# Strassen's sums and products put into one order on two engines of a decoder kernel

## The chip, the cores and the metric

The kernel runs on one core of a Trainium2 chip. What counts is the device time of one execution in microseconds (us). A core has a matrix engine (PE), whose weight loads are told apart as PEld, three engines for elementwise work (VectorE, DVE; ScalarE, ACT; GpSimd, POOL) and a queue for transfers (SyncE, SP). Each engine works through its instructions in order. Where the program doesn't write an order out, a scheduler sets that of DVE, ACT, POOL and SP from priorities when the program is built.

## The reference

The reference computes two layers of a decoder on 256 tokens of width 1024. Each layer has a feed-forward network (FFN), a mixer and a second FFN, all followed by a layer norm. All arrays are float32. The change touches the FFNs alone; there are four.

```python
D_MODEL, SEQ, DEPTH, D_FF = 1024, 256, 2, 2816
def _swiglu(x, w1, w3, w2):
    return (jax.nn.silu(x @ w1) * (x @ w3)) @ w2
for l in range(DEPTH):
    h = _swiglu(x, ffn_w1[l, 0], ffn_w3[l, 0], ffn_w2[l, 0])
    x = _layernorm(ALPHA * x + 0.5 * h, ln_g[l, 0], ln_b[l, 0])
    h = _mixer(x, l, ...)
    x = _layernorm(ALPHA * x + h, ln_g[l, 1], ln_b[l, 1])
    h = _swiglu(x, ffn_w1[l, 1], ffn_w3[l, 1], ffn_w2[l, 1])
    x = _layernorm(ALPHA * x + 0.5 * h, ln_g[l, 2], ln_b[l, 2])
```

## The kernel before

**Numbers in two parts.** A float32 operand is split into a high part, which ACT copies into the rounded type (`whi`, L188 or L238), and a low part, which DVE finds as the number less its high part (`wlo`, L190 or L240). Each product is then three matmuls: high by high, low by high, high by low. The weights of both parts are made afresh from raw tiles of 128 x 2048 (1 MB), which SP loads (L164 for a tile in two halves, L166 for a whole one). `stream` (L169) does this for a tile: it loads it and issues, for each half of 1024 columns, the high part and the low part. `pieces` (L349) does it for a tile that is on chip already, through `split` (L236). The high and the low parts rotate through pools of eight buffers each (`hi_pool`, `lo_pool`).

**The front of an FFN.** silu(x w1) * (x w3) is made in blocks n = 0 to 4 of 512 columns, with two more columns of tiles (k = 16 and 17) by `gemm_a2`. Block 0 goes first, by `gemm_first` (L471) in the first FFN and by `gemm_b2` in the others. Then the loop at L875 goes through the blocks 1, 2 and 4 in twelve units of 24 matmuls (PE, L274). Between these units block 3 is made by Strassen's algorithm: the generator `seven` (L825) makes seven products of 12 matmuls each (PE, L362), and after the units 1, 2, 4, 6, 8, 9 and 10 the loop takes the next one (L887). PE's order is thus written out by hand. The products work on four quarters of the weights, w11, w12, w21 and w22, each a raw tile. They are, in this order: the first on w11; the crossed one on w21; the third on w11+w12; the fourth on that +w22; the fifth on w22; the sixth on w12+w22; the seventh on w11+w12+w22+w21, all up to sign conventions in the sums of x. The tiles of raw numbers are r1 (w11, then sums), r2 (w12, in two buffers of `hi_pool`) and r3 (w22, in two of `lo_pool`). Sums come about in two ways: `plus` (L344) adds two tiles on DVE, in two operations of 128 x 1024 (L346); `gather` (L338) issues two accumulating loads from POOL's queue (L341), which add the weights in memory onto the tile on chip. In the front, `plus` makes w11+w12 and +w22 in r1, and `gather` makes r2 = w12+w22 and the last r1 (+w21). The results are put together on DVE (L851, L852 and others); `sums_of_x` (through `strassen_sums`, L814 to L823, whose sums are L818) makes the sums of x on the side.

**The way to w2.** When a block is done, `turned` (L774) transposes it: `transposed` (L222) parts the two 16-bit halves of the numbers (L205 on ACT, L207 on POOL), a transfer from SP's queue transposes them (L211), and `joined` (L214) brings the halves together again, on ACT (L218) or on another engine (L220). Then the block is split into `h_hi` and `h_lo`. For blocks 3 and 4 the parting and the joining both run on ACT.

**The second weight, w2.** `gemm_seven` (L366) makes part of h w2 by Strassen's algorithm too, again seven products (PE, L362), and between them `between()` takes the streamed rest of the weights (PE, L391). There are `plus` and `gather` for the sums as in the front (`spare` stands for r2 and r3). Each product that goes into the residual is taken out of its bank by `ln.fold` (L593, on DVE), and the next product into that bank waits for it. At the end `held = list(rest(1))` (L434) streams the last weights, and the blocks of the second half follow.

**Small things beside.** `setup` (L527), started in the first front after its block 1 (n, t) = (1, 0) at L762, loads tables and the tokens from POOL's queue (L537), and after 12 beats (a beat is about the PE time of a unit's quarter) it issues a second part: small DVE operations and an Exp on ACT (L547), which changes ACT's table. `behind(ins)` (L148) makes an instruction be issued after another one on its engine; `beside(task, delay)` starts a side task in a number of beats.

Of the kernel before, what the change touches and what calls it, by code (L numbers as in the profile page):

```python
# [11 lines left out]
F32 = mybir.dt.float32  # L12
# [4 lines left out]
AF = mybir.ActivationFunctionType  # L17
# [37 lines left out]
def trunk(ctx, tc, x, xT, w13a, w13b, w2, wb, wqk, wu, wg, wgr, wbr, wbrr, wo, gateb, gatebr, sgug, sgub, sguwT, sgubias, lam, diffg,  # L55
# [28 lines left out]
    def slots(s, n, dtype=F32):  # L84

        return [act.tile([P, 512], dtype, tag="slot", name=name(s)) for _ in range((n + 1) // 2)]
# [58 lines left out]
    gate, behind_norm, sooner = [], [None], []  # L145
    latest, added, emptied, silu, turned_by, loaded, spread = [None, None], [None], [None], [None], [None], [None], [None]

    def behind(ins):  # L148

        return tc.issue_after(ins) if ins is not None else nullcontext()  # L150
# [18 lines left out]
    def stream(src, width=CH, sub=HC, lent=(), after=(None, None), pool=()):  # L169

        raw = fetch(src, width)
        out = []
        first = sooner.pop() if sooner else latest
        for o in range(0, width, HC):
            eng = G if o // HC in pool else V
            if o // HC in lent:
                hi, lo = ([act.tile([P, 512], F32R, tag="slot", name=name(n)) for _ in range(2)] for n in ("lhi", "llo"))
                at = [(hi[j], lo[j]) for j in range(2)]  # L180
            else:
                hi = hi_pool.tile([P, HC], F32R, tag="hi", name=name("whi"))
                lo = lo_pool.tile([P, HC], F32R, tag="lo", name=name("wlo"))
                at = [(hi[:, p : p + sub], lo[:, p : p + sub]) for p in range(0, HC, sub)]
            for p, (h, w) in zip(range(0, HC, sub), at):
                r = raw[:, o + p : o + p + sub]
                with behind(first[0]):
                    A.activation(h, r, AF.Copy)  # L188
                with behind(after[o // HC] or (first[1] if eng is V else None)):
                    eng.tensor_tensor(out=w, in0=r, in1=h.bitcast(F32), op=ALU.subtract)  # L190
            out.append((hi, lo))
        return out

# [149 lines left out]

    def plus(raw, more):  # L344
        for v, m in zip(halved(raw), halved(more)):
            V.tensor_tensor(out=v, in0=v, in1=m, op=ALU.add)  # L346
        return raw

    def pieces(raw):  # L349
        out = []  # L350
        for v in halved(raw):
            hi = hi_pool.tile([P, HC], F32R, tag="hi", name=name("whi"))
            lo = lo_pool.tile([P, HC], F32R, tag="lo", name=name("wlo"))
            split(hi, lo, v)
            out.append((hi, lo))
        return out

# [8 lines left out]
    def gemm_seven(src, xh, xl, sums, spare, ln, done):  # L366

        q = [[bank(), bank()], [side_bank(), bank()]]
        bx, bz = side_bank(), q[1][0]
        (w11, w21), (w12, w22) = ([s[:, o : o + CH] for o in (0, CH)] for s in src)

        def rest(c):  # L380
            for k in range(8, FT, 4):
                nk = min(4, FT - k)
                for j, piece in enumerate(stream(src[c][:, k * 512 : (k + nk) * 512], nk * 512)):
                    yield k + 2 * j, piece

        def rows(t, c, k0, piece, o=0, n=512):
            for j in range(2):
                k = k0 + j
                hi, lo = (w[:, j * 512 + o : j * 512 + o + n] for w in piece)
                for m, (y, x) in enumerate(((hi, xh), (lo, xh), (hi, xl))):  # L390
                    PE.matmul(q[c][t][:, :n] if o == 0 else more[:, :n], x(k, t), y,  # L391
                              start=k == 8 and m == 0 and (c, t) != (1, 0), stop=k == FT - 1 and m == 2, skip_group_check=True)
            beat(n / 1024)

        def block(t, k0):
            return tuple(lambda k, f=f: f(k0 + k, t) for f in (xh, xl))

        a11, a12, a22 = block(0, 0), block(0, 4), block(1, 4)
        first = rest(0)

        def between():
            k, piece = next(first)
            for t in range(NT):
                rows(t, 0, k, piece)

        r1 = fetch(w11)
        p1 = pieces(r1)
        r2 = fetch(w12, raw=spare[0])
        plus(r1, r2)
        product(bx, a11, p1, True, False)  # L410
        ln.fold(0, 0, bx, ALU.add, True)
        between()
        product(q[0][0], a12, pieces(fetch(w21)), False, False)
        gather(r2, w22)
        r3 = fetch(w22, raw=spare[1])
        between()
        product(bz, sums[0], pieces(r1), True, False)
        ln.fold(1, 1, bz, ALU.add, True)
        between()
        product(bx, sums[1], pieces(plus(r1, r3)), False, False)  # L420
        ln.fold(0, 1, bx, ALU.subtract, True)
        gather(r1, w21)
        between()
        product(bz, sums[3], pieces(r3), False, False)
        between()
        product(bx, sums[2], pieces(r2), False, False)
        ln.fold(1, 1, bx, ALU.subtract, False)
        between()
        product(bx, a22, pieces(r1), False, True)
        ln.fold(1, 0, bx, ALU.add, True)  # L430
        between()
        for t in range(NT):
            done(t, q[0][t], 0, 512)
        held = list(rest(1))  # L434
        cuts = ((0, 512),), (((0, 256), (256, 256)) if ln.last else ((0, 512),))
        for t in range(NT):
            for o, n in cuts[t]:
                more = bank() if o else None
                for k, piece in held:
                    rows(t, 1, k, piece, o, n)  # L440
                done(t, (more if o else q[1][t])[:, :n], 512 + o, n)
# [85 lines left out]
    def setup(after):  # L527
# [3 lines left out]
        for dst, src in ((x_tok[0], x[:P, :]), (x_tok[1], x[P:, :]), (cos_t, cosT), (sin_t, sinT), (dgs, diffg),  # L531
# [3 lines left out]
                first = first[:, 0]  # L535
            V.tensor_copy(first[:, :1], after)
            G.dma_start(dst, src)  # L537
        yield 12
        with behind(added[0]):
            V.tensor_scalar(out=gbh, in0=gbh, scalar1=0.5, scalar2=None, op0=ALU.mult)  # L540
        pr = s512("lampr").rearrange("p (l f d) -> p l f d", l=DEPTH, f=4)[:, :, :2]
# [189 lines left out]
    def ffn(l, f, i, norm, last=False):  # L731
# [14 lines left out]
        def front(n, wait):  # L746
# [10 lines left out]
            def done(t, ps):  # L757
                p = tiles[t]
                s = p[:, 1]
                added[0] = V.tensor_tensor(out=s, in0=s, in1=ps, op=ALU.mult).ins  # L760
                beside(turned(n, t, s, p[:, 0], wait[t]), 0)
                if norm is None and (n, t) == (1, 0):  # L762
                    beside(setup(s[:, :1]), 0)
            return gate_, done

# [8 lines left out]
        def turned(n, t, s, p, wait):  # L774
            lead = 3.5 if n == 0 and norm else 0
            to = slots("held", 2)[0] if n < 2 else p
            yield from transposed(s, p, s, lead, wait - lead, 2.6, A, to, A if n else G)
            yield 0.6
            if n < 2:
                held[n, t] = to  # L780
# [44 lines left out]
        def seven(src, x_sums):  # L825
# [3 lines left out]
            (w11, w21), (w12, w22) = ([v[:, o : o + CH] for o in (0, CH)] for v in src)  # L829
            bx, bz, bq = (side_bank() for _ in range(3))  # L830
            g0, v0, v1, g1 = (slots("seven", 2)[0] for _ in range(4))
            r1 = fetch(w11)
            product(bx, x11, pieces(r1), True, False)
            A.activation(g0, bx, AF.Copy)
            yield
            product(bq, x12, pieces(fetch(w21)), True, True)
            V.tensor_tensor(out=g0, in0=bq, in1=g0, op=ALU.add)
            A.activation(g0, g0, AF.Silu)
            r2 = fetch(w12, raw=[hi_pool.tile([P, HC], F32, tag="hi", name=name("r2")) for _ in range(2)])
            yield  # L840
            product(bz, x_sums[0], pieces(plus(r1, r2)), True, False)
            A.activation(v1, bz, AF.Copy)
            gather(r2, w22)
            r3 = fetch(w22, raw=[lo_pool.tile([P, HC], F32, tag="lo", name=name("r3")) for _ in range(2)])
            yield
            product(bx, x_sums[1], pieces(plus(r1, r3)), False, False)
            A.activation(v0, bx, AF.Copy)
            gather(r1, w21)
            yield
            product(bz, x_sums[3], pieces(r3), False, True)  # L850
            V.tensor_tensor(out=v0, in0=bz, in1=v0, op=ALU.subtract)  # L851
            V.tensor_tensor(out=g0, in0=g0, in1=v0, op=ALU.mult)  # L852
            beside(turned(3, 0, g0, v0, 6.3), 0)
            yield
            product(bx, x_sums[2], pieces(r2), False, False)
            V.tensor_tensor(out=v1, in0=v1, in1=bx, op=ALU.subtract)
            yield
            product(bx, x22, pieces(r1), False, True)
            A.activation(g1, bx, AF.Silu)
# [8 lines left out]
        if norm is None:  # L868
            gemm_first(w13(0), both_done(0, (8.3, 8.3)))
            beside(sums_of_x(), 1)  # L870
        else:
            gemm_b2(w13(0), xh, xl, both_done(0, (11.3, 8.3)), norm=norm)
            beside(sums_of_x(), 5)
        products, unit = seven(w13(3), x_sums), 0
        for n in (1, 2, NB - 1):  # L875
            ps = [[bank() for _ in range(2)] for _ in range(NT)]
            ready = front(n, (7.3, 6.3) if n < NB - 1 else (9.3, 8.3))
            for c in range(2):
                for m in range(2):
# [4 lines left out]
                        if c:  # L884
                            ready[m](t, ps[t][m])
                    unit += 1
                    if unit in (1, 2, 4, 6, 8, 9, 10):  # L887
                        next(products)
        for j in range(FA, FT - 4, 2):
            for m, z in gemm_a2([w13a[l, f, j - FA + m] for m in range(2)], both, lambda m: t512("silu")):  # L890
# [405 lines left out]
```

## Time and profile before

| | us |
|---|---|
| median of three runs | 1207.35 |
| lowest and highest | 1205.91, 1212.65 |
| the profiled execution | 1206.38 |
| its span in the profile | 1204.6 |
| mean granted clock of PE | 0.998 |

The profile is that of one execution. A row of a timeline has the start in us, the duration, the engine, the line of the program, the operation, "output<-inputs" by the names of the tiles, the shapes, and the number of instructions that the row holds (x4: four of the same kind one after another, whose duration is that of all). Square brackets give the engine's idle time just before and what ended it. Matmuls are pipelined: the duration of one overlaps the next. A row of the waits names who waited, for whom, and the total in us, the count and the longest. A row of a group by line gives the shortest, the mean and the longest in ns. A row of windows gives the window, its length, and the busy time of each engine in it.

### The profile page before, as it was taken

To read this page: it belongs to the slowest core of one execution; us is meant where nothing else is said; L and a number is where in the kernel's file an instruction comes from. 1 tells how busy PE (TensorE), PEld (TensorE's weight loads), DVE (VectorE), ACT (ScalarE), POOL (GpSimd) and SP (SyncE) were. 2 spreads that over 40 slices of the span, in tenths; PEclk is the share of its full clock that TensorE was granted. 3 is DMA by queue.
4 is the path that set the end of the run, shared out by engine and by line. 5 is a ranking of instruction groups with operands and counts; after the bars stand their busy time and mean duration, and the time that the engine had idled before them with its cause. 6 is when DMAs were issued, how large, how long until landed. Compare 5 with 4: busy or idle time off the path is not lost.

```text
span 1204.6 us, 16667 instructions
## 1 busy us (share of the span) xinstructions
PE 1184.8 (98%) x5771; PEld 993.6 (82%) x5771; DVE 998.5 (83%) x1548; ACT 842.4 (70%) x1452; POOL 227.7 (19%) x334
## 2 busy tenths in 40 slices
PE   8999989999999999999999999999999999999998
PEld 7887878888888887888788888788888888888876
DVE  6779878887778987898898798888965989978985
ACT  6589747568964684996576996576788556679870
POOL 1220101146530211001020000003564112110000
PEclk9999999999999999999999999999999999999999
DMA  9998884767855758879768889676666755897970
GB/s 347 298 276 250 235 304 166 254 227 201 252 190 184 252 175 253 245 271 238 260 205 261 216 296 237 233 262 245 203 209 209 253 188 154 274 236 239 288 220 35
DMA packets 130660, 281.39 MB, mean 234 GB/s; under 512 B 89184, under 2 KB 90256, under 8 KB 106000
## 3 DMA queue, kind: packets, MB, share of 16 engines
q1 hardware_dynamic: 121392, 248.80, 62.7%
q0 software_dynamic: 8752, 31.00, 11.5%
q8 instruction: 45, 0.74, 0.2%
q10 hardware_dynamic: 432, 0.52, 0.1%
q14 instruction: 39, 0.32, 0.1%
HBM read 254.35 MB, written 1.05 MB: 212 GB/s over the span
## 4 chain that ended last, share of the span: by engine, by line
PE 80%; issue 7%; DMA 7%; DVE 3%; ACT 1%; POOL 1%; SPq 0%; POOLq 0%; DVEq 0%; ACTq 0%
PE bank L274 42%; PE bank L286 13%; PE sbank L362 7%; PE bank L293 6%; PE bank L391 4%; DMA raw<-in_w 3%; PE sbank L391 3%; DVE wlo L190 2%; DMA r<-in_w13b 2%; PE bank L500 1%; PE sbank L955 1%; DMA raw<-in_w13b 1%; ACT whi L238 1%; PE sbank L1011 1%; PE sbank L1129 1%
## 5 line engine op out<-in xcount | busy, mean ns | idle before, releaser
L190 DVE TENSOR_TENSOR wlo<-raw,whi 128x1024 fp32r<-128x1024 f32 (+1 forms) x374 | 413.8, 1135 | 59.0 <-ACT whi L188 45.9
L188 ACT ACTIVATE whi<-raw 128x1024 fp32r<-128x1024 f32 (+1 forms) x378 | 350.0, 958 | 129.0 <-PE bank L274 38.0
L274 PE MATMUL bank<-whi,x 128*128 128x512 f32 x1224 | 386.3, 390 | 0.0
L274 PEld LDWEIGHTS bank<-whi,x 128*128 128x128 f32 x1224 | 229.8, 188 | 47.4
L274 PE MATMUL bank<-wlo,x 128*128 128x512 f32 x612 | 238.7, 390 | 1.8 <-DVE wlo L190 1.7
L286 PE MATMUL bank<-x,whi 128*128 128x512 f32 x640 | 153.3, 391 | 0.0
L286 PEld LDWEIGHTS bank<-x,whi 128*128 128x128 f32 x640 | 118.2, 188 | 23.8
L274 PEld LDWEIGHTS bank<-wlo,x 128*128 128x128 f32 x612 | 114.9, 188 | 26.9 <-DVE wlo L190 3.5
L240 DVE TENSOR_TENSOR wlo<-raw,whi 128x1024 fp32r<-128x1024 f32 (+1 forms) x96 | 109.4, 1153 | 13.2 <-ACT whi L238 9.7
L238 ACT ACTIVATE whi<-raw 128x1024 fp32r<-128x1024 f32 (+1 forms) x96 | 92.4, 980 | 25.4 <-DMA raw<-in_w 15.3
L293 PEld LDWEIGHTS bank<-x,wlo 128*128 128x128 f32 x640 | 81.4, 191 | 2.9
L293 PE MATMUL bank<-x,wlo 128*128 128x256 f32 x640 | 82.6, 283 | 0.0
L391 PE MATMUL bank<-whi,hhi 128*128 128x512 f32 (+1 forms) x182 | 68.2, 375 | 0.0
L391 PE MATMUL bank<-whi,hlo 128*128 128x512 f32 (+1 forms) x182 | 67.9, 373 | 0.0
L391 PE MATMUL bank<-wlo,hhi 128*128 128x512 f32 (+1 forms) x182 | 67.9, 373 | 0.0
L205 ACT ACTIVATE planes<-planes 128x512 uint16<-128x512 uint16 x48 | 27.5, 619 | 27.3 <-DVE planes L760 27.0
L931 POOL TENSOR_TENSOR swap<-swap,sin_t 128x512 f32<-128x512 f32 x16 | 26.6, 1661 | 100.1 <-DMA swap<-z 48.3
L341 POOL DMA_DIRECT2D spare<-in_w x8 | 6.8, 851 | 204.5 <-DVE raw L346 203.5
L294 ACT ACTIVATE r<-bank 128x256 f32<-128x256 f32 x96 | 34.5, 371 | 15.6 <-PE bank L293 15.5
L362 PE MATMUL sbank<-whi,xhs 128*128 128x512 f32 x128 | 42.0, 389 | 0.0
L391 PEld LDWEIGHTS bank<-whi,hlo 128*128 128x128 f32 x182 | 34.3, 188 | 6.1
L391 PEld LDWEIGHTS bank<-wlo,hhi 128*128 128x128 f32 x182 | 34.3, 188 | 6.0
(285 smaller groups left out, 2141.0 us busy)
## 6 DMA issues: line engine op xcount, KB each, us to landing
raw<-in_w13b SPq DMA_DIRECT2D x68, 1024.0 KB, 7.0
raw<-in_w SPq DMA_DIRECT2D x32, 1024.0 KB, 5.7
raw<-in_wb SPq DMA_DIRECT2D x16, 1024.0 KB, 6.4
raw<-in_wqk SPq DMA_DIRECT2D x16, 1024.0 KB, 6.3
r<-in_w13b SPq DMA_DIRECT2D x16, 512.0 KB, 7.7
raw<-in_w13a SPq DMA_DIRECT2D x8, 1024.0 KB, 4.8
raw<-in_wgr SPq DMA_DIRECT2D x8, 1024.0 KB, 5.1
raw<-in_wg SPq DMA_DIRECT2D x8, 1024.0 KB, 5.0
```

Of the source, the lines that this page charges most:

```text
L188: A.activation(h, r, AF.Copy)
L190: eng.tensor_tensor(out=w, in0=r, in1=h.bitcast(F32), op=ALU.subtract)
L205: A.activation(o, i, AF.Copy)
L238: a = A.activation(hi, src, AF.Copy).ins
L240: return a, eng.tensor_tensor(out=lo, in0=src, in1=hi.bitcast(F32), op=ALU.subtract).ins
L274: PE.matmul(ps, xx, w, start=start and n == 0, stop=stop and n == 2)
L286: PE.matmul(b[-1], hi[:, k * P : (k + 1) * P], xc(k), start=k == 0, stop=False)
L293: PE.matmul(b[n][:, :T], lo[:, k * P : (k + 1) * P], xc(k)[:, :T], start=False, stop=k == KT - 1)
L294: emptied[0] = A.activation(r[:, s], b[n][:, T:], AF.Copy, scale=scale).ins
L362: PE.matmul(ps, x[o](k), y, start=start and k == n == 0, stop=stop and k == 3 and n == 2, skip_group_check=True)
L391: PE.matmul(q[c][t][:, :n] if o == 0 else more[:, :n], x(k, t), y, start=k == 8 and m == 0 and (c, t) != (1, 0), stop=k == FT - 1 and m == ...
L931: turned_by[0] = G.tensor_tensor(out=s3, in0=s3, in1=s, op=ALU.mult).ins
```

## The change

`line` holds the last instruction of the order on ACT, that on DVE, and whether the order is on. It is switched on after block 0 of each front and off after `held = list(rest(1))` in `gemm_seven`. While it is on, each high part of `stream` and of `pieces` is issued on ACT after the one before it, and each low part and each operation of `plus` on DVE after the one before it, in the order in which the program makes them. Other instructions are not in the order: the folds (L593), the silus, the joined copies, the results of products (L851, L852), the sums of x (L818), the splits of h.

In each front `gather(r2, w22)` becomes `plus(r2, r3)`. In the first front the products are taken after the units 2, 4, 6, 8, 9, 10 and 11, the crossed product moves from second to sixth place with its tile in a buffer r4, and `gather(r1, w21)` becomes `plus(r1, r4)`. `setup` starts after (2, 0), its second part after 16 beats. The joined copies of blocks 3 and 4 go to POOL. In `gemm_seven` the calls of `gather` stay.

```diff
+    line = [None, None, False]
+
+    def inline(eng, ins):
+        if line[2]:
+            line[eng is V] = ins
+        return ins
...
-                with behind(first[0]):
-                    A.activation(h, r, AF.Copy)
-                with behind(after[o // HC] or (first[1] if eng is V else None)):
-                    eng.tensor_tensor(out=w, in0=r, in1=h.bitcast(F32), op=ALU.subtract)
+                with behind(first[0]), behind(line[0]):
+                    inline(A, A.activation(h, r, AF.Copy).ins)
+                with behind(after[o // HC] or (first[1] if eng is V else None)), behind(line[1] if eng is V else None):
+                    low = eng.tensor_tensor(out=w, in0=r, in1=h.bitcast(F32), op=ALU.subtract).ins
+                if eng is V:
+                    inline(V, low)
...
     def plus(raw, more):
         for v, m in zip(halved(raw), halved(more)):
-            V.tensor_tensor(out=v, in0=v, in1=m, op=ALU.add)
+            with behind(line[1]):
+                inline(V, V.tensor_tensor(out=v, in0=v, in1=m, op=ALU.add).ins)
...
-            split(hi, lo, v)
+            for eng, ins in zip((A, V), split(hi, lo, v, after=line[:2])):
+                inline(eng, ins)
...
         held = list(rest(1))
+        line[:] = None, None, False
...
-        yield 12
+        yield 16
...
-                if norm is None and (n, t) == (1, 0):
+                if norm is None and (n, t) == (2, 0):
...
-            yield from transposed(s, p, s, lead, wait - lead, 2.6, A, to, A if n else G)
+            yield from transposed(s, p, s, lead, wait - lead, 2.6, A if n < 3 else G, to, A if n else G)
...
+            def crossed(raw):
+                product(bq, x12, pieces(raw), True, True)
+                V.tensor_tensor(out=g0, in0=bq, in1=g0, op=ALU.add)
+                A.activation(g0, g0, AF.Silu)
+
+            def first_row():
+                V.tensor_tensor(out=g0, in0=g0, in1=v0, op=ALU.mult)
+                beside(turned(3, 0, g0, v0, 6.3 if norm else 4), 0)
...
-            product(bq, x12, pieces(fetch(w21)), True, True)
-            V.tensor_tensor(out=g0, in0=bq, in1=g0, op=ALU.add)
-            A.activation(g0, g0, AF.Silu)
+            if norm:
+                crossed(fetch(w21))
             r2 = fetch(w12, raw=[hi_pool.tile([P, HC], F32, tag="hi", name=name("r2")) for _ in range(2)])
-            yield
+            if norm:
+                yield
...
-            gather(r2, w22)
...
-            gather(r1, w21)
+            if norm:
+                gather(r1, w21)
             yield
+            plus(r2, r3)
             product(bz, x_sums[3], pieces(r3), False, True)
             V.tensor_tensor(out=v0, in0=bz, in1=v0, op=ALU.subtract)
-            V.tensor_tensor(out=g0, in0=g0, in1=v0, op=ALU.mult)
-            beside(turned(3, 0, g0, v0, 6.3), 0)
+            if norm:
+                first_row()
             yield
             product(bx, x_sums[2], pieces(r2), False, False)
             V.tensor_tensor(out=v1, in0=v1, in1=bx, op=ALU.subtract)
+            if not norm:
+                yield
+                r4 = fetch(w21)
+                crossed(r4)
+                first_row()
+                plus(r1, r4)
...
+        line[:] = None, None, True
         products, unit = seven(w13(3), x_sums), 0
...
-                    if unit in (1, 2, 4, 6, 8, 9, 10):
+                    if unit in ((1, 2, 4, 6, 8, 9, 10) if norm else (2, 4, 6, 8, 9, 10, 11)):
```

## The prediction

> **What bounds the kernel now.** I read the page's head first, then the waits of PE, then the timelines of PE, DVE and ACT around each wait.
>
> ```profile
> span 1204.6 us, 16667 instructions
> PE 1184.8 (98%) x5771; PEld 993.6 (82%) x5771; DVE 998.5 (83%) x1548; ACT 842.4 (70%) x1452; POOL 227.7 (19%) x334
> PE sbank L362 <- DVE xtok L593: 6.9, 4, 3.1
> PE bank L274 <- DVE wlo L190: 1.7, 2, 1.1
> PE sbank L362 <- DVE wlo L240: 1.6, 1, 1.6
> ```
>
> PE is busy for 98% of the span and its work is not changed: a gain can only come out of its few waits (total us, count, longest). Those in this change's reach are the four of L593, the folds that must empty a bank before the seventh product of w2, and three for low parts, L190 and L240, in the fronts.
>
> Front 1, PE and DVE before its sixth product:
>
> ```profile
> 91.47 0.68 DVE L851 TENSOR_TENSOR seven<-sbank,seven 128x512 f32<-128x512 f32 x1
> 92.07 0.68 DVE L818 TENSOR_TENSOR held<-held,held 128x512 f32<-128x512 f32 x1
> 92.67 0.68 DVE L852 TENSOR_TENSOR seven<-seven,seven 128x512 f32<-128x512 f32 x1
> 94.11 1.22 DVE L240 TENSOR_TENSOR wlo<-r,whi 128x1024 fp32r<-128x1024 f32 x1
> 93.20 0.61 PE L362 MATMUL sbank<-whi,xhs 128*128 128x512 f32 x2
> 95.39 0.50 PE L362 MATMUL sbank<-wlo,xhs 128*128 128x512 f32 x1 [1.57 <-DVE wlo L240]
> 35.11 2.72 PE sbank L362 x12
> ```
>
> The last row, of the chain of waits, is the undisturbed pace: 2.72/12 = 0.227 us a matmul. Two matmuls from 93.20 make the third due at 93.65; it came at 95.39, 1.74 late, because the product's second low part stood on DVE behind small operations of other work, three of them shown. Fronts 2 and 4:
>
> ```profile
> 479.94 1.22 DVE L346 TENSOR_TENSOR raw<-raw,r 128x1024 f32<-128x1024 f32 x1 [5.83 <-DMA r<-in_w13b]
> 480.62 0.61 PE L274 MATMUL bank<-whi,x 128*128 128x512 f32 x2
> 482.36 0.50 PE L274 MATMUL bank<-wlo,x 128*128 128x512 f32 x1 [1.13 <-DVE wlo L190]
> 1071.35 0.61 PE L274 MATMUL bank<-whi,x 128*128 128x512 f32 x2
> 1072.51 0.50 PE L274 MATMUL bank<-wlo,x 128*128 128x512 f32 x1 [0.55 <-DVE wlo L190]
> ```
>
> Here DVE's head was the sum r1+r3, which sat 5.83 us waiting for the load of r3 while the streamed tile's low part, already possible, stood behind it. Late: 482.36 − 481.07 = 1.29 and 1072.51 − 1071.80 = 0.71. Front 3 has no such row.
>
> The w2 stage of the first FFN, DVE and PE:
>
> ```profile
> 123.27 1.22 DVE L190 TENSOR_TENSOR wlo<-raw,whi 128x1024 fp32r<-128x1024 f32 x1 [0.55 <-ACT whi L188]
> 124.41 2.35 DVE L346 TENSOR_TENSOR raw<-raw,spare 128x1024 f32<-128x1024 f32 x2
> 144.88 0.50 PE L362 MATMUL sbank<-wlo,sum 128*128 128x512 f32 x1 [0.59 <-DVE bc L559]
> 159.04 4.62 DVE L190 TENSOR_TENSOR wlo<-raw,whi 128x1024 fp32r<-128x1024 f32 x4
> 163.58 0.68 DVE L593 SCALAR_TENSOR_TENSOR xtok<-xtok,sbank 128x512 f32<-128x512 f32 x1
> 164.41 0.62 PE L362 MATMUL sbank<-whi,hhi 128*128 128x512 f32 x1 [3.06 <-DVE xtok L593]
> 164.83 0.63 PE L362 MATMUL sbank<-wlo,hhi 128*128 128x512 f32 x1
> 167.81 0.47 PE L362 MATMUL sbank<-whi,hlo 128*128 128x512 f32 x1
> ```
>
> The fold came after four streamed low parts (4.62). After the 3.06 us of idling the matmuls start 0.42 apart: the ninth at 167.81 is 3.40 behind the first where eight paces make 1.81, so 1.6 more is lost. The second FFN's w2, on ACT, DVE and PE:
>
> ```profile
> 554.56 2.35 DVE L346 TENSOR_TENSOR raw<-raw,spare 128x1024 f32<-128x1024 f32 x2
> 555.36 2.67 ACT L218 ACTIVATE planes<-planes 128x512 uint16<-128x512 uint16 x4 [4.72 <-DMA planes<-planes]
> 558.41 1.04 ACT L238 ACTIVATE whi<-raw 128x1024 fp32r<-128x1024 f32 x1
> 572.59 1.06 ACT L238 ACTIVATE whi<-raw 128x1024 fp32r<-128x1024 f32 x1 [5.02 <-DMA raw<-in_w]
> 574.82 4.62 DVE L190 TENSOR_TENSOR wlo<-raw,whi 128x1024 fp32r<-128x1024 f32 x4
> 579.36 0.68 DVE L593 SCALAR_TENSOR_TENSOR xtok<-xtok,sbank 128x512 f32<-128x512 f32 x1
> 580.19 0.47 PE L362 MATMUL sbank<-whi,hhi 128*128 128x512 f32 x1 [0.96 <-DVE xtok L593]
> ```
>
> Read backwards: PE at 580.19 waits for the fold, the fold for four low parts, these stand behind the seventh product's parts, whose high part (572.59) waited for an accumulating load of r1; that load could start only when the fourth product's parts of r1 were taken, the first of them at 558.41, when ACT had finished four joined copies of block 4 (555.36 to 558.03), which had kept it 4.72 us idle at its head. The fourth product's first sum was done at 554.56 + 1.22 = 555.78, the second at 556.91.
>
> **The change part by part.** The sum stands against the profiled run's 1206.4 us (span 1204.6 and 1.8 around it), 1.0 under the median 1207.35.
>
> *a) Strict order on ACT and DVE.* It reorders and adds no instruction. In fronts 2 and 4 the sum r1+r3 goes behind the streamed low parts: −1.29 and −0.71. In front 1 the late low part was held by L851, L852 and L818, which are not put in the order; but there the order of products is changed too, and the setup work that shared this place is moved by a unit, so I count −1.74. Together −3.7; bounds 0 and −3.7.
>
> *b) Sums on DVE in place of loads.* r2+r3 is two operations in each front, and the first front also gets r1+r4: 4×2+2 = 10, at 1.22 each (479.94) 12.2 us. What hides them:
>
> ```profile
> 29.50:116.50 87.00, 85.27 (x374) 69.64 (x373) 69.03 (x87) 67.83 (x91) 14.62 (x17) 1.00 0.97 275
> 513.88 1.22 DVE L190 TENSOR_TENSOR wlo<-raw,whi 128x1024 fp32r<-128x1024 f32 x1
> 517.86 0.39 PE L274 MATMUL bank<-wlo,x 128*128 128x512 f32 x1
> ```
>
> In the window over front 1 (length; busy PE, PEld, DVE, ACT, POOL; clock; DMA share; GB/s) DVE has 87.00 − 69.03 = 18 us free. The shortest lead I found away from the late places is 517.86 − 515.10 = 2.76 us, over the 2.44 of a pair. Cost 0; were the cover gone, 2.44 per front, 12.2 in all. r3 is on chip by then, since the fourth product summed it, so no new load is waited for. In the first front r1 keeps its buffer to the end and r4 is fetched later; both are sums of tiles that a product before them has already read.
>
> *c) Loads removed.* Ten accumulating half-tile loads (512 KB each), from POOL's queue. None is waited for by PE now, so 0 on the path; front 1, where DMA is 0.97 busy, loses 2 MB, so its loads can only land earlier. The w2 stages keep theirs.
>
> *d) Joined copies of blocks 3 and 4 from ACT to POOL.* 32 copies:
>
> ```profile
> L218 ACT ACTIVATE planes<-planes x32: 755/762/801, 102.4 to 1147.2; 128x512 uint16<-128x512 uint16 x32
> L220 POOL COPY gr<-gr x8: 769/1130/1245, 395.4 to 996.1; 128x512 uint16<-128x512 uint16 x8
> 26.81 2.36 DVE L190 TENSOR_TENSOR wlo<-raw,whi 128x1024 fp32r<-128x1024 f32 x2 [1.70 <-ACT whi L188]
> 29.68 2.77 DVE L240 TENSOR_TENSOR wlo<-raw,whi 128x1024 fp32r<-128x1024 f32 x2
> 29.83 3.09 POOL L207 COPY planes<-planes 128x512 uint16<-128x512 uint16 x2 [23.78 <-DVE planes L760]
> ```
>
> ACT is freed of 32×0.76 = 24 us; POOL, 19% busy, takes 32×1.13 = 36 (by 29.83 up to 1.55 each). The w2 chain above decides. If ACT then takes the fourth product's high part before block 4's split, it starts near 555.8 and not at 558.41, up to 2.6 earlier; if it keeps the split ahead, it waits for POOL's four copies, 4×1.13 = 4.5 to 4×1.55 = 6.2 against 2.67, so 1.9 to 3.5 later. Between these I take the three later w2 stages as unchanged, 0, because the order is fixed without knowing which transfer is late: half may go either way.
>
> *e) w2 of the first FFN.* The strict order puts its first sum (124.41) ahead of the streamed low parts that it now follows (123.27), and block 3's copies leave ACT just before. I let its fold wait fall to the mean of the other three: (6.9 − 3.06)/3 = 1.3, a gain of 1.8; an idle of 1.57 (95.39) was followed by no half pace, so the 1.6 goes too, and the 0.59 at 144.88: −4.0. Bounds 0 and −5.3 (3.06+1.6+0.59).
>
> *f) POOL's copies beside DVE.* Two low parts took 2.77 beside 3.09 of POOL copying, 2.36 without: +0.41. Half of four copies lies beside each w2 chain, so about 0.25, four times: +1.0 (bounds 0 and 1.6). [...]
>
> Sum: 1206.4 − 3.7 + 0 + 0 + 0 − 4.0 + 1.0 = 1199.7.
>
> **Rivals.**
> *Up*: ACT takes the fourth product's high part as soon as its sum is there; the chain is 2.6 earlier and all fold waits go: 1206.4 − 3.7 − 6.9 − 1.6 − 0.6 = 1193.6. For: those copies are ACT's only 4.7 us idle there. Against: the split of block 4 may keep its place.
> *Fronts only*: w2 is as before, since its gathers and folds are untouched: 1202.7.
> *Order misses*: the change doesn't do what it says; front 1's late low part still stands behind unlisted operations and w2 stays, while POOL costs its 1.0: 1206.4 − 2.0 + 1.0 = 1205.4. Against: front 1's products are moved.
> [...]
> *Slower*, the other side: ACT keeps block 4's split ahead of the fourth product's high part and POOL's copies run at 1.55, so in each w2 the chain is 3.5 later, 14.0; the fold waits of the three later stages then pass 3 us and each gets the 1.6 of half pace, 4.8; the first stage gains nothing: 1206.4 − 3.7 + 14.0 + 4.8 = 1221.5. It decides from the point where the split stands first; from there each us of POOL copying beyond 2.67 is lost four times. For: in the trace before, the copies (555.36) do stand first. Against: the scheduler then sees a ready high part beside a split that waits for a slower engine.
>
> **How the numbers follow.** Forecast 0.37 (own range 1196.5 to 1202.5: a, e and f at half their bounds), up 0.18, fronts only 0.15, order misses 0.05, lock 0.05, slower 0.20. The range 1192 to 1212 holds all but slower. I call 0.5%, 6 us, the least that a measurement tells from no change: faster means under 1201.3, slower over 1213.4. Faster: 0.26 of the forecast's 0.37, up's 0.18, 0.04 of fronts only, 0.48. Slower: 0.20. Same: the rest, 0.32.
>
> **What would show it.** a) PE has no wait for L190 or L240 in the fronts, and no sum there shows an idle time for r. b) L346 has ten more instructions in the fronts, and no lead falls under 1 us. c) POOL shows no load into r in the fronts. d) The rows of L220 on POOL have 32 more copies: their mean, and whether the fourth product's high part comes before or after them, settles d) and the rivals. e) The first w2's fold wait is near 1.3 with no half pace behind it. f) Low parts beside copies take 1.4, not 2. The forecast is wrong if any w2 waits over 3 us for its fold.

## The result, and the profile after

The changed kernel takes 1207.36 us (median of 12 runs, 1204.47 to 1212.67), the kernel before 1207.84 (12 runs on the same chip, 1199.43 to 1216.19). The ratio is 0.9999, 95% interval 0.9972 to 1.0027: no difference that can be measured. I had predicted 1199.7. The profiled execution of the changed kernel took 1212.67 us, the slowest of its 12, so its stages can show more than the usual loss.

The head of the page and the waits of PE and DVE, changed kernel:

```profile
span 1211.0 us, 16633 instructions
PE 1190.9 (98%) x5771; PEld 998.5 (82%) x5771; DVE 1014.4 (84%) x1558; ACT 822.9 (68%) x1418; POOL 299.8 (25%) x356
PE sbank L373 <- DVE xtok L605: 9.6, 4, 3.3
PE sbank L373 <- DVE wlo L249: 2.4, 2, 1.5
DVE raw L356 <- DMA spare<-in_w: 16.8, 9, 3.4
```

The row for low parts on L274 (now L283) is gone: from 21 us on, the fronts have no wait of PE at all. The folds' row has grown from 6.9 to 9.6 us. The last row is new in size: DVE waits 16.8 us, in its sums, for the loads into `spare`. Before:

```profile
DVE raw L346 <- DMA spare<-in_w: 1.5, 2, 1.2
```

PE has the same 5771 matmuls in both kernels, and little but matmuls sets the end. So the start of the same matmul in two traces can be compared, and how their difference grows over a stretch is what the stretch won or lost. I worked this out from the traces for all kernels, in us against the profiled execution before, one execution of each. The columns of fronts 2 and 4 hold the mixer ahead of them. Left out are the first 21 us, which vary by -1.2 to +1.5, the third front (0.03 at most; +1.09 in experiment 5) and the last 10 us:

| kernel | front 1 | w2, 1st FFN | front 2 | w2, 2nd | w2, 3rd | front 4 | w2, 4th | w2, 2nd to 4th |
|---|---|---|---|---|---|---|---|---|
| changed | -2.64 | -2.27 | -1.45 | +6.53 | +4.38 | -0.84 | +3.21 | +14.1 |
| 1 no order in w2 | -2.64 | -1.95 | -1.45 | -0.30 | -0.41 | -0.84 | +2.54 | +1.8 |
| 2 joins on ACT | -2.64 | -4.61 | -1.41 | +4.29 | +4.80 | -0.84 | +3.08 | +12.2 |
| 3 sum after chunk | -2.64 | -2.11 | -1.41 | +0.05 | +0.30 | -0.84 | +2.41 | +2.8 |
| 4 only joins on POOL | -0.09 | -3.30 | -1.45 | +4.01 | +0.41 | -0.70 | +0.27 | +4.7 |
| 5 one edge in w2 | -0.11 | -0.75 | +0.40 | +6.13 | +2.04 | +0.54 | +4.91 | +13.1 |
| 6 order in fronts only | -1.11 | -2.42 | -1.43 | -0.63 | +1.60 | -0.84 | +2.18 | +3.2 |
| 7 gathers in fronts | -2.64 | -1.61 | -1.41 | +1.53 | +2.88 | -0.84 | +0.57 | +5.0 |
| 8 no order at all | -2.64 | -0.73 | -1.41 | +1.62 | +0.18 | -0.84 | +0.31 | +2.1 |
| 9 load behind | -2.64 | -2.88 | -1.44 | +0.69 | +0.69 | -0.84 | +0.42 | +1.8 |
| 10 no order, load behind | -2.64 | -2.71 | -1.45 | +4.26 | +1.44 | -0.84 | +5.11 | +10.8 |

The first row is the whole story: the fronts won 4.9 us, the first w2 2.3, and the three later w2 stages gave back 14.1, of which 1.7 to 2.7 each is half pace after the fold's wait. This is the slowest execution of the 12, though, and 6.3 us above the profiled one before. The medians are equal, so a typical execution gives back about as much as it wins, some 7 us: an estimate, with the wins of 4.9 and 2.3 taken as the same in every execution. Row 10 is also that of the slowest of its 12 runs. Where the loss begins is seen in the second FFN, before, on DVE and SP (the transposes of block 4 are the last row):

```profile
536.72 1.22 DVE L190 TENSOR_TENSOR wlo<-raw,whi 128x1024 fp32r<-128x1024 f32 x1
538.68 1.23 DVE L190 TENSOR_TENSOR wlo<-raw,whi 128x1024 fp32r<-128x1024 f32 x1 [0.74 <-ACT whi L188]
539.86 2.53 DVE L346 TENSOR_TENSOR raw<-raw,spare 128x1024 f32<-128x1024 f32 x2
539.93 0.33 SPq L166 DMA_DIRECT2D raw<-in_w  x1
546.11 0.33 SPq L166 DMA_DIRECT2D spare<-in_w  x1
546.49 7.61 SPq L211 DMA_TRANSPOSE planes<-planes  x2
```

And in the changed kernel, with POOL, ACT and PE:

```profile
533.38 2.42 DVE L356 TENSOR_TENSOR raw<-raw,spare 128x1024 f32<-128x1024 f32 x2 [2.79 <-DMA spare<-in_w]
535.72 2.35 DVE L197 TENSOR_TENSOR wlo<-raw,whi 128x1024 fp32r<-128x1024 f32 x2
538.10 0.33 SPq L173 DMA_DIRECT2D raw<-in_w  x1
539.75 0.33 SPq L173 DMA_DIRECT2D spare<-in_w  x1
540.13 11.11 SPq L220 DMA_TRANSPOSE planes<-planes  x2
552.58 3.77 POOL L229 COPY planes<-planes 128x512 uint16<-128x512 uint16 x4 [15.41 <-DMA planes<-planes]
555.03 0.63 ACT L247 ACTIVATE hhi<-planes 128x512 fp32r<-128x512 f32 x1 [10.52 <-POOL planes L229]
555.57 1.05 ACT L247 ACTIVATE whi<-raw 128x1024 fp32r<-128x1024 f32 x1
577.77 0.76 PE L373 MATMUL sbank<-whi,hhi 128*128 128x512 f32 x1 [3.34 <-DVE xtok L605]
580.46 0.63 PE L373 MATMUL sbank<-whi,hhi 128*128 128x512 f32 x1
580.89 0.63 PE L373 MATMUL sbank<-wlo,hhi 128*128 128x512 f32 x1
```

PE is 6.36 us earlier here, so 6.36 is taken off the times of before. The two low parts of chunk 0, the first streamed tile of w2, ended at 533.55 before and end at 538.07 now, 4.5 later: the order has put them behind the sum r1+r2, and the sum sits 2.79 us at DVE's head for its load, then takes 2.4. The second low part frees a raw buffer, so SP's load of the next streamed tile (1 MB) goes out at 538.10 in place of 533.57. That load had landed, at 544.89, before r3's load (546.11) and the transposes were issued; now it is issued ahead of them on the same queue, and r3's load takes 11.7 us from its issue to landing instead of 8.2. r3's load and the transposes are issued as before (546.11 and 546.49 less 6.36 are 539.75 and 540.13), but from the transposes' issue to the first joined copy pass 552.58 - 540.13 = 12.45 us instead of 555.36 - 546.49 = 8.87. All that I had traced backwards from the fold is late by 3.5 to 3.9 against PE: the fourth product's parts, the accumulating load, the seventh product's parts, the fold. The fold's wait goes from 0.96 to 3.34, and half pace follows it (0.43 us between the last two rows, as against 0.227; the granted clock is 0.50 from 576.43 us on).

### The profile page after: what moved, and what is told of

The parts are those of the page before. It is cut to its first block, busy times and chain, and to the rows that moved or that the text cites. A ratio compares the mean times of both kernels' runs of the same rounds, so it can differ in the third digit from the quotient of the medians.

```text
span 1211.0 us, 16633 instructions
## 1 busy us (share of the span) xinstructions
PE 1190.9 (98%) x5771; PEld 998.5 (82%) x5771; DVE 1014.4 (84%) x1558; ACT 822.9 (68%) x1418; POOL 299.8 (25%) x356
## 4 chain that ended last, share of the span: by engine, by line
PE 87%; DMA 8%; DVE 2%; issue 2%; POOL 1%; ACT 1%; SPq 0%; POOLq 0%; DVEq 0%; ACTq 0%
PE bank L283 45%; PE bank L295 15%; PE sbank L373 8%; PE bank L302 7%; PE bank L402 4%; DMA planes<-planes 4%; DMA raw<-in_w 3%; PE sbank L402 3%; PE bank L512 2%; DVE wlo L197 1%; PE sbank L984 1%; POOL planes L229 1%; PE sbank L1040 1%; PE sbank L1158 1%; ACT whi L247 0%
## 5 line engine op out<-in xcount | busy, mean ns | idle before, releaser
L283 PE MATMUL bank<-whi,x 128*128 128x512 f32 x1224 | 386.3, 390 | 0.0
L283 PEld LDWEIGHTS bank<-whi,x 128*128 128x128 f32 x1224 | 229.8, 188 | 47.9
L283 PE MATMUL bank<-wlo,x 128*128 128x512 f32 x612 | 238.2, 389 | 0.0
L283 PEld LDWEIGHTS bank<-wlo,x 128*128 128x128 f32 x612 | 114.9, 188 | 23.1
L229 POOL COPY seven<-seven 128x512 uint16<-128x512 uint16 x16 | 64.8, 4110 | 106.0 <-ACT whi L195 83.2
L719 POOL COPY nvia<-ntwo 128x256 uint16<-128x256 uint16 x20 | 10.0, 546 | 153.6 <-DMA ntwo<-nvia 113.6
L402 PEld LDWEIGHTS bank<-whi,hhi 128*128 128x128 f32 x182 | 34.7, 191 | 6.2
```

Of the source, the lines that this page charges most:

```text
L229: eng.tensor_copy(out=o, in_=i)
L283: PE.matmul(ps, xx, w, start=start and n == 0, stop=stop and n == 2)
```

## The experiments

My theory ('order') was that chain. The rivals were that POOL's joined copies make the loss ('copies', the mechanism of my rival "slower"), and that w2 gives back whatever the fronts win ('given back'). The experiments are numbered as in the table. Ratios are to the kernel before, on the same chip; 1 to 4 were timed together, and so were 5 to 8, and 9 with 10.

**1. The order off in w2.**

```diff
+        line[:] = None, None, False
         gemm_seven([w2[l, f, c] for c in range(2)], hh, hl, sums, spare, ln, done)
```

> The strict order is on in the fronts only, and off in all of w2; the rest is as in the changed kernel. Theory 'order': the loss in w2 comes from the sum r1+r2, which the order puts at DVE's head ahead of chunk 0's low parts, where it waits 2.8 us for its load; these low parts, and with them a raw buffer and the load into it, are 4.5 us late, and that load collides with r3's load and the transposes of block 4. Then the three later w2 stages lose about 0 against before (in the changed kernel +6.5, +4.4, +3.2), the fronts keep their gain of 4.9, and the first w2 is as before or better: 1199 to 1203, ratio to before 0.992 to 0.997. Theory 'copies' (the joined copies on POOL delay the fourth product): the later w2 stages still lose 3 to 6 us each, about 1207. Theory 'given back' (loads come no earlier, so what the fronts gain returns as waits in w2): PE's w2 stages still lose about 5 us in all, 1205 to 1207.

Measured: 1201.11 us, ratio 0.9944 (0.9916 to 0.9972). The later w2 stages lose 1.8 instead of 14.1, and the fronts keep all of their 4.9. 'Given back' falls.

**2. The joined copies back on ACT.**

```diff
-            yield from transposed(s, p, s, lead, wait - lead, 2.6, A if n < 3 else G, to, A if n else G)
+            yield from transposed(s, p, s, lead, wait - lead, 2.6, A, to, A if n else G)
```

> The changed kernel with the joined copies of blocks 3 and 4 back on ACT. 'Order': the w2 stages lose as in the changed kernel, fold waits near 3 us in the three later ones: 1205 to 1210, ratio 0.998 to 1.003. 'Copies': the loss of 14 us in the three later w2 stages goes, 1193 to 1196, ratio 0.988 to 0.991. 'Given back': as 'order'.

Measured: 1206.22 us, ratio 0.9997 (0.9970 to 1.0024); the later w2 stages still lose 12.2. 'Copies' falls.

**3. The sum r1+r2 of w2 written behind chunk 0**, order on everywhere.

```diff
-        plus(r1, r2)
         product(bx, a11, p1, True, False)
         ln.fold(0, 0, bx, ALU.add, True)
         between()
+        plus(r1, r2)
```

> The changed kernel, order on everywhere, but in w2 the sum r1+r2 is written (and so ordered) behind chunk 0's low parts. 'Order': the three later w2 stages are as before the change, chunk 0's low parts leave without the 2.8 us wait, the raw load is issued 4 us earlier: 1194 to 1202, ratio 0.989 to 0.996. 'Copies' and 'given back': 1205 to 1209.

Measured: 1202.67 us, ratio 0.9951 (0.9924 to 0.9978). Moving one line recovers most of it, the order staying on: it is not the order as such, but the place that it gives to this sum.

**4. The kernel before, with the joined copies on POOL alone.**

```diff
-            yield from transposed(s, p, s, lead, wait - lead, 2.6, A, to, A if n else G)
+            yield from transposed(s, p, s, lead, wait - lead, 2.6, A if n < 3 else G, to, A if n else G)
```

> The kernel before with nothing changed but the joined copies of blocks 3 and 4 on POOL. 'Order': no change, between -2 and +2 us, since the fourth product's high part comes 3.0 us after the transposes land either way: ratio 0.998 to 1.002. 'Copies': the three later w2 stages lose 3 to 6 us each, +10 to +14 us, ratio 1.008 to 1.012. 'Given back': no change.

Measured: 1207.36 us, ratio 1.0002 (0.9974 to 1.0030), as 'order' said. Its second w2 lost 4.0 in the profiled execution, some 1.7 of it by half pace; the two others 0.4 and 0.3. Its rows in that w2, POOL, ACT and SP:

```profile
541.59 9.78 SPq L211 DMA_TRANSPOSE planes<-planes  x2
552.75 4.02 POOL L220 COPY planes<-planes 128x512 uint16<-128x512 uint16 x4 [11.91 <-DMA planes<-planes]
555.43 0.63 ACT L238 ACTIVATE hhi<-planes 128x512 fp32r<-128x512 f32 x1 [8.75 <-POOL planes L220]
555.97 1.04 ACT L238 ACTIVATE whi<-raw 128x1024 fp32r<-128x1024 f32 x1
```

The fourth product's first high part begins 3.2 after the first copy; with the copies on ACT it was 558.41 - 555.36 = 3.05, and 555.57 - 552.58 = 2.99 in the changed kernel. The waits in fronts 2 and 4 are gone here too, with no order and no sum changed; a) below takes this up.

**5. The kernel before with one edge added:** chunk 0's two low parts behind the sum.

```diff
+    summed = [None]
...
-            V.tensor_tensor(out=v, in0=v, in1=m, op=ALU.add)
+            summed[0] = V.tensor_tensor(out=v, in0=v, in1=m, op=ALU.add).ins
...
-                for j, piece in enumerate(stream(src[c][:, k * 512 : (k + nk) * 512], nk * 512)):
+                late = summed[0] if (c, k) == (0, 8) else None
+                for j, piece in enumerate(stream(src[c][:, k * 512 : (k + nk) * 512], nk * 512, after=(late, late))):
```

> The kernel before with one thing added: in w2, chunk 0's two low parts are issued behind the sum r1+r2; no other order, joined copies on ACT, loads into r in the fronts as before. 'Order': this edge alone makes the loss of the changed kernel's later w2 stages, 3 to 6 us each, with fold waits of 2.5 to 3 us: 1213 to 1221, ratio to before 1.005 to 1.011, unless the schedule of the fronts moves too and loses its waits (then 1 to 4 us less). If the loss needs the full order or the copies on POOL: within 2 us of before, ratio 0.998 to 1.002.

Measured: 1216.79 us, ratio 1.0066 (1.0036 to 1.0095). The edge alone makes the loss: 13.1 us in the later w2 stages of the profiled execution, and by the ratio of all runs 0.66% of 1209.4, or 8.0 us. Its rows on DVE, SP and ACT in the second FFN repeat those of the changed kernel:

```profile
539.57 2.46 DVE L347 TENSOR_TENSOR raw<-raw,spare 128x1024 f32<-128x1024 f32 x2 [4.14 <-DMA spare<-in_w]
541.95 2.35 DVE L191 TENSOR_TENSOR wlo<-raw,whi 128x1024 fp32r<-128x1024 f32 x2
544.33 0.33 SPq L167 DMA_DIRECT2D raw<-in_w  x1
545.24 11.21 SPq L212 DMA_TRANSPOSE planes<-planes  x2
557.72 2.68 ACT L219 ACTIVATE planes<-planes 128x512 uint16<-128x512 uint16 x4 [7.41 <-DMA planes<-planes]
```

557.72 - 545.24 = 12.48 from the transposes' issue to the joined copies, with these on ACT.

**6. The kernel before with the order in the fronts only.** The edit is that of `line` in `stream`, `plus` and `pieces` as in the change, switched off ahead of `gemm_seven`; products, setup, gathers and joined copies are as before.

> The kernel before with the strict order in the fronts and nothing else (products of front 1, setup, sums, joined copies as before). 'Order fixes fronts 2 and 4': the waits for low parts at 482 and 1072 go, -2.3 us; front 1's wait of 1.7 (a low part behind L851, L852 and L818) stays, as those are not in the order: 1204 to 1206, ratio 0.997 to 0.999. If the order reaches front 1 too, about 5 us less, as in the run with the order in the fronts only: ratio 0.994 to 0.997.

Measured: 1203.16 us, ratio 0.9948 (0.9920 to 0.9976), the second case of what I wrote. Fronts 2 and 4 have no wait; front 1 kept a wait of 0.5 of its 1.57 us for the product's low part. Whether the order itself does that in front 1, or only a schedule that came out otherwise, isn't shown.

**7. As 1, with `gather(r2, w22)` in place of the sum in the fronts.**

```diff
+            gather(r2, w22)
             r3 = fetch(w22, raw=[lo_pool.tile([P, HC], F32, tag="lo", name=name("r3")) for _ in range(2)])
...
-            plus(r2, r3)
             product(bz, x_sums[3], pieces(r3), False, True)
```

> As the run without the order in w2, but r2 = w12+w22 is made by the accumulating loads again, in all four fronts. If the ten, here eight, sums on DVE cost nothing and the loads removed were hidden: the same as that run, 1199 to 1203, no wait for low parts in the fronts in either. If the sums cost DVE time that PE feels: faster than that run by up to 8 times 1.2 = 9.8 us. If the loads' traffic was in the way: slower by some us, with waits for DMA in the fronts.

Measured: 1203.45 us, ratio 0.9946 (0.9918 to 0.9973), that of 1 within its interval. All fronts are the same as in 1 to 0.1 us: neither these eight sums nor the loads that they replace cost PE anything there. The two operations of r1+r4 in the first front stayed.

**8. The changed kernel with the order off everywhere.**

```diff
-        line[:] = None, None, True
```

> The changed kernel with the order off everywhere: the new products of front 1, the sums, the moved setup and the joined copies on POOL stay. If the order is what ends the fronts' waits: those of fronts 2 and 4 come back (2.3 us), w2 as in the run without the order in w2, 1202 to 1205. If the joined copies' move to POOL alone ends them, as the run with that alone showed by a schedule without the two waits: fronts have no wait, 1199 to 1203. The later w2 stages lose nothing by either.

Measured: 1201.55 us, ratio 0.9930 (0.9905 to 0.9956). All of the fronts' gain is there without the order, and w2 loses 2.1. By the ratios this and 1 are the fastest that I have, half a per cent below both kernels; 3, 6 and 7 can't be told from them by their intervals.

**9. The changed kernel, order on everywhere, with the late load sent behind the transposes.**

```diff
-    line = [None, None, False]
+    line, sent_last, hold = [None, None, False], [None], [None]
...
-        with behind(gate[0][1] if gate and gate[0][0] < 0 else None):
+        with behind(gate[0][1] if gate and gate[0][0] < 0 else None), behind(hold[0]):
...
-        return nc.sync.dma_start(out.bitcast(U16).rearrange("p (k t) -> p k t", t=P), src.bitcast(U16),
-                                 transpose=True).ins
+        sent_last[0] = nc.sync.dma_start(out.bitcast(U16).rearrange("p (k t) -> p k t", t=P), src.bitcast(U16),
+                                         transpose=True).ins
+        return sent_last[0]
...
                 nk = min(4, FT - k)
+                hold[0] = sent_last[0] if (c, k) == (0, 16) else None
```

> The changed kernel, order on everywhere; the one load in w2 that had become late (the third streamed tile, 1 MB) is issued behind the transposes of block 4 instead of ahead of r3's load. 'Collision' (that load shares the DMA with r3's load and the transposes and makes both 3.5 us late, and by them the fourth product and the fold): r3 and block 4 land about 3.5 us sooner against PE, the later w2 stages lose 0 to 2 us each instead of 3 to 6: 1197 to 1203, ratio 0.991 to 0.996. 'Low parts' (the late low parts themselves, through buffers or DVE's backlog, make the loss): fold waits stay near 3 us, 1205 to 1209, ratio 0.998 to 1.001.

Measured: 1201.95 us, ratio 0.9965 (0.9948 to 0.9982); the kernel before ran at 1206.75 beside it. The ratio is a hair outside what I wrote for 'collision' (0.991 to 0.996), the time is inside. Its rows on DVE, SP, POOL and PE:

```profile
533.04 2.46 DVE L357 TENSOR_TENSOR raw<-raw,spare 128x1024 f32<-128x1024 f32 x2 [2.96 <-DMA spare<-in_w]
539.22 0.33 SPq L173 DMA_DIRECT2D spare<-in_w  x1
539.65 7.84 SPq L220 DMA_TRANSPOSE planes<-planes  x2
548.81 4.59 POOL L230 COPY planes<-planes 128x512 uint16<-128x512 uint16 x4 [11.93 <-DMA planes<-planes]
573.99 0.47 PE L374 MATMUL sbank<-whi,hhi 128*128 128x512 f32 x1 [1.65 <-DVE xtok L607]
574.30 0.40 PE L374 MATMUL sbank<-wlo,hhi 128*128 128x512 f32 x1
```

The sum still waits 2.96 us and the low parts are still late, but from the transposes' issue to the copies pass 548.81 - 539.65 = 9.16, near the 8.87 of before, and the later w2 stages lose 1.8 instead of 14.1. So the late low parts cost little by themselves; the load that they held back does, by its collision. This rests on the profiles: the intervals of this ratio and of the changed kernel's (0.9972 to 1.0027) overlap.

The collision can be counted over all the kernels. In the three later w2 stages the first joined copy begins 10.8 to 13.2 us after the transposes' issue where a streamed tile's load is still under way at that issue (the changed kernel with 12.45, 12.15 and 11.22, 2 and 5, nine stages), and 8.3 to 11.2 us after it where none is (the other nine kernels, among them the kernel before with 8.87, 9.30 and 8.69). The two ranges meet, so a transfer can be that slow without this load too.

**10. Both, 8 and 9.**

> The changed kernel with the order off everywhere, and the third streamed tile's load behind the transposes. If r3 and the transposes are what the fourth product waits for in this schedule too, they land sooner and the fold waits (7.8 us in all without order) shrink by half or more: 1194 to 1199, ratio 0.986 to 0.991. If that load was done before them anyway, as in the kernel before: as without it, ratio 0.991 to 0.995. If the tile itself then comes too late for its matmuls: slower than that, with waits of L402 in w2.

Measured: 1202.99 us, ratio 0.9965 (0.9940 to 0.9989): nothing is won over 8. In the profiled execution the fold waited longer than in 8 (12.1 us in all against 7.8) and the transposes of the second FFN took longer from issue to copies (10.5 against 9.4). It was the slowest of the 12 runs, 7.1 us over their median. Why its transfers were slower is not settled; no streamed tile's load stood ahead of them.

## Why the prediction was wrong, point by point

**a) Strict order.** The sum for the fronts held: forecast -3.7, measured -4.9 (-2.64, -1.45, -0.84; some 0.9 of small waits behind the one at 95.39, which I left out, is in it). But this is the step that failed: "It reorders and adds no instruction", with bounds of 0 and -3.7. In these traces a place in an engine's queue is a wait for all behind it. I had seen just this in fronts 2 and 4, a sum at DVE's head that waits for a load (5.83 us in front 2) with a ready low part behind it. In e) I even wrote that the order puts w2's first sum ahead of the streamed low parts; I counted that as a gain of the first w2 and did not ask what the sum waits for, nor what the same place costs in the three later w2 stages. There the sum waits 2.8, 3.4 and 2.3 us with chunk 0's low parts behind it. Price: 14.1 us in the three later w2 stages in the profiled execution, with 13.1 for the edge alone by experiment 5; by the ratios of all runs 6.6 (0.9944 in 1 against 0.9999) and 8.0.

The fronts, too, got rid of their waits in more than one way. The sum r1+r3 of front 2 in the changed kernel, in 4 and in 8:

```profile
475.59 1.22 DVE L356 TENSOR_TENSOR raw<-raw,r 128x1024 f32<-128x1024 f32 x1
474.56 1.23 DVE L346 TENSOR_TENSOR raw<-raw,r 128x1024 f32<-128x1024 f32 x1 [3.90 <-DMA r<-in_w13b]
472.44 1.23 DVE L356 TENSOR_TENSOR raw<-raw,r 128x1024 f32<-128x1024 f32 x1 [2.42 <-DMA r<-in_w13b]
```

With the order it comes behind the streamed low parts and waits for nothing, as I had forecast. In 4 and 8 it still stands at DVE's head with a low part behind it, and waits 3.90 and 2.42 us instead of 5.83; but it begins 1.9 and 3.4 us sooner against PE than before, and so the low part is in time. The load of r3 was issued at the same point and landed sooner, in one execution of each. I have no cause for that: in 8 the accumulating loads of the fronts are gone, in 4 they aren't. So the order is a way to end these waits and not the only one, and what they cost hangs on when that load lands.

**b) and c) Sums for loads.** Right: 0 on the path, by experiment 7, for eight of the ten operations. The sign that I set under a) came only in part: two sums in front 1 still wait for r (4.2 us in all, against 19.6 before), at no cost to PE.

**d) Joined copies on POOL.** 0 was right in the total, by experiments 2 and 4, for another reason than mine; the first w2 may be an exception (see e). I let ACT's split wait for four copies, "1.9 to 3.5 later". It waits for the two of its own tile: in the changed kernel it starts at 555.03, 2.45 after the first copy, while the third is running. The bound of 3.5 a stage, on which the rival "slower" rested, was thus too wide.

**e) The first w2.** Forecast -4.0, measured -2.27. The fold's wait went from 3.06 to 0.70 and the half pace went, more than I had counted, but the fourth product now waits there for its parts (0.5 for a high part and 1.5 for a low one, against 0.59). That can't be put down to the collision of the later stages: in this stage a streamed tile's load stood ahead of the transposes in the kernel before, too, and from their issue to the first copy passed 11.8 us (127.64 to 139.48) against 12.7 now (125.00 to 137.71). In 9, where that load goes behind, 7.9 us pass, and PE waits the same 1.53 us. ACT, POOL and PE in the first w2 of 9:

```profile
133.01 8.46 POOL L230 COPY planes<-planes 128x512 uint16<-128x512 uint16 x4 [9.92 <-DMA planes<-planes]
140.14 0.63 ACT L248 ACTIVATE hhi<-planes 128x512 fp32r<-128x512 f32 x1 [9.44 <-POOL planes L230]
143.80 0.50 PE L374 MATMUL sbank<-wlo,sum 128*128 128x512 f32 x1 [1.53 <-DVE wlo L250]
```

There the four copies take 8.46 us instead of 3.94 in the changed kernel's first w2, and the split of block 4, with the product's parts behind it, waits for the first two of them. In 2, with the copies on ACT, the product doesn't wait and the stage wins 4.6 us. So d) may have cost some 2 us here, where I had put it at nothing; with one execution of each this stays open.

**f) POOL beside DVE.** The 1.0 can't be seen apart. Of the copies that I priced at 1.13, those of block 4 took 1.02 us in the mean and those of block 3 4.11, one of them 14.45 beside a long run of DVE's, as told below.

**The rivals.** "Slower" had a loss in the same three stages, 10.5 and 4.8 for half pace against the 14.1 of the profiled execution, on the wrong mechanism; with the fronts' gain and the first w2's it ended at no change. Its place (the fourth product's inputs late, the folds past 3 us) was the right one to look at, and the sign that I had set, a w2 that waits over 3 us for its fold, came (3.34). "Up" did not happen: the split of block 4 kept its place before the fourth product's high part. The range did hold the time, but by luck: a gain and a loss that I hadn't seen cancelled. No row here shows a DVE that POOL's copies stop ("lock", 0.05): two sums that met them took 2.87 us (136.79) instead of 2.35. What was wrong was the claim of a gain.

## What to carry to other kernels

When an order is fixed by hand, go through every instruction in it that waits for a transfer and ask what is queued behind it: here the price was not the wait of 2.79 us but the buffer that was freed 4.5 us late, and the load that then went out on top of others. A gain in one stage and a loss in another cancel in the total, so compare the start of the same matmul in both traces stage by stage before explaining a zero. If an edit ends a wait, try it without the part that it is named after.

## What the runs showed of the hardware that I had not expected

**One of POOL's copies lasted 14.45 us beside DVE's work.** The joined copies of block 3 in the changed kernel, a group by line (x16, busy, mean ns), their spread, and two rows of the timeline:

```profile
L229 POOL COPY seven<-seven 128x512 uint16<-128x512 uint16 x16 | 64.8, 4110 | 106.0 <-ACT whi L195 83.2 <-DMA seven<-seven 22.8
L229 POOL COPY seven<-seven x16: 771/1773/14453, 109.4 to 1127.9; 128x512 uint16<-128x512 uint16 x16
511.61 16.09 POOL L229 COPY seven<-seven 128x512 uint16<-128x512 uint16 x2
525.81 1.27 DVE L249 TENSOR_TENSOR wlo<-raw,whi 128x1024 fp32r<-128x1024 f32 x1 [0.38 <-ACT whi L247]
```

One copy, of a kind whose shortest takes 0.77 us, lasted 14.45 (the first of the two at 511.61): it ended at 526.06, just after DVE's first pause since it had begun (0.38, before 525.81). That DVE's work held the copy is my reading of this one execution; no run sets the two apart. It cost nothing, since block 3 isn't needed until w2; the copies at 133.01 in experiment 9, shown under e), are needed at once. In f) I had priced DVE's side alone, its 0.41; here it is the copy that takes longer. DVE loses too, but less: in the first w2 of the changed kernel two sums that met copies took 2.87 us (136.79) instead of 2.35.

**Half pace came behind some of PE's longer idle times, not behind all.** The granted clock in the traces has half pace as 0.50. From 60 us on, up to the last stage, the profile before has it once, from 164.56 us on for 3.41 us, 0.15 behind the fold's wait of 3.06. That of the changed kernel has it three times: from 576.43 for 6.83 us, within the wait of 3.34, and from 760.75 and 1177.18 for 3.41 us each, 1.0 behind the starts after waits of 2.81 and 2.73. No other idle time of 0.5 us or more in these two stretches, the longest of 1.57 us (before 95.39, in the kernel before), has half pace behind it.

The length of one idle time doesn't settle it. In the first w2 of experiment 5 matmuls start 0.43 us apart (146.33, 146.76) shortly after an idle time of 0.76 (before 145.52) and one of 1.23 ahead of that. In experiment 8 half pace came in the first w2, and none behind the longest of its fold waits, 2.56 us in the second w2 (window, length, then the busy time of PE, PEld, DVE, ACT and POOL, the clock, DMA share and GB/s):

```profile
161.44:164.85 3.41, 3.41 (x9) 2.65 (x9) 2.26 (x3) 1.13 (x2) 0.00 (x0) 0.50 1.00 399
577.86:581.28 3.42, 3.42 (x17) 2.81 (x16) 2.79 (x4) 1.76 (x3) 0.00 (x0) 1.00 1.01 410
```

In the kernel before and in the changed one a stretch of half pace holds for 8 or 12 matmuls, 0.43 us apart instead of 0.227, some 1.6 to 2.7 us of loss. So a fold wait of 2 to 3 us cost that much more in one stage and nothing more in another, which is part of why single stages in the table above scatter. What decides it is not shown.
